# Two output products as pairs of 64-row matmuls in a hybrid decoder step

## The chip, the cores and the metric

The kernel runs on one core of a Trainium2 chip. The time is that of one execution on the device, in microseconds (us). Times of engines, waits and transfers come from one profiled execution. The engines are PE (matrix products; its weight loads are listed as PEld), DVE and ACT (element-wise work, both can read the accumulator memory PSUM), POOL (element-wise work in SBUF) and SP (which issues most DMAs).

## The reference

One inference step of a two-layer decoder trunk in float32, for one prompt of 512 tokens and for 8 sample sequences of 8 tokens each; the model width is 1024. Cut to what matters:

```python
# layer 0
xr, yg = split(h @ rnn_w_in, 2)
xr = causal_dwconv(xr)                                  # width 4
o = rg_lru(xr)                                          # gates, then a recurrence over the tokens
x = x + g1 * ((o * gelu(yg)) @ rnn_w_out)               # output product of the recurrent block
x = x + g2 * swiglu(modulate(rms_norm(x)))
kv = modulate(rms_norm(x)) @ w_kv                       # shared keys and values
# layer 1
q = rope(modulate(rms_norm(x)) @ attn_w_q)
x = x + g1 * (sliding_sink_attention(q, k, v) @ attn_w_o)   # output product of the attention
x = x + g2 * swiglu(modulate(rms_norm(x)))
y = rms_norm(x)
```

Shift, scale and gate of each norm (`sh`, `sc`, `g`) come from a conditioning vector through a large product (`ada`). The outputs are the two `y`, and the convolution, recurrence and key/value states.

## The kernel before, in words

The residual stream is kept transposed, model columns on partitions and tokens along the free dimension: `x[h]` with 8 blocks (`KC`) of 128 model columns. The tokens are in two column halves `h` (called A and B), each of 288 columns (`HC`): 256 prompt tokens (`HP`) and 4 sample sequences of 8 tokens.

A product with float32 accuracy is made from three products in the reduced type float32r. Each operand v is split into `hi`, v rounded to float32r, and `lo`, v - hi rounded; `product` (lines 1032 to 1040) adds hi x hi, hi x lo and lo x hi for each of the 8 blocks of 128 rows: 24 matmuls of 128 rows, 128 weight columns and 288 token columns, all into one PSUM bank. Weights arrive by DMA as `raw`, and ACT and DVE split them into two `wh` buffers (`convert`, line 1006). `linear` (line 1049) makes a job of such a product and an evacuation function, for one block of 128 output columns; each job runs once per column half.

The two output products of the change are of this kind: 8 jobs with `rnn_w_out` (line 1214), whose moving operands are pairs of `sl` buffers, and 8 jobs with `attn_w_o` (line 1814), whose moving operands lie in `h`. Their evacuation is `residual` (line 1058): one DVE instruction multiplies 256 columns of the bank with the gate and adds them to `x`, a second multiplies the 32 sample columns, POOL adds those, and ACT squares the new block for the next norm. After the last block the norm of that half follows (`norm_f`, line 918), and then the SwiGLU products.

PSUM has eight banks: six for products and transposes (`NMM`, tag `mm`), two for the `ada` products and the attention outputs. `td` is a set of four scratch buffers of SBUF.

No instruction is issued when the Python code reaches it. Every call is recorded (line 489, which is why all instructions carry that line), with a cost from a table (`Engine.record`, lines 430 to 489). `Recorder.schedule` (line 227) is a planner: it plays the five engines against each other, takes for each the recorded instruction that can start first with a bonus for those early in the code, and may look ahead of the oldest one that is still open by `WIN` places. It knows banks and buffers in use, and adds 100 ns where PE goes from one matmul `mode` to another (line 339). The resulting order is written out engine by engine; on the chip each engine runs its list in order and waits for semaphores.

Matmuls of fewer than 128 rows exist already in one place that matters here: the attention scores (line 1623) take 64 rows of a head from the upper or the lower half of the partitions, two by two, in plain float32.

Of the kernel before, what the change touches and what calls it, by code (L numbers as in the profile page):

```python
# [13 lines left out]
F32R = mybir.dt.float32r  # L14
BF16 = mybir.dt.bfloat16
AF = mybir.ActivationFunctionType
ALU = mybir.AluOpType
AX = mybir.AxisListType

P = 128  # L20
D = 1024
KC = D // P
# [5 lines left out]
HC = 288  # L28
# [18 lines left out]
MK = "4 V VVG S VVG"  # L47
MQ = "4 V VVG SSSV VG"
SPW = 60
WIN = 600  # L50

RNN = "x0 x1 x2 g0 g1 x3 y0 y1 x4 g2 g3 x5 y2 x6 y3 g4 g5 x7 y4 y5 g6 g7 y7 y6"
ATT = "q0A q2A a0A q1A q0B a2A q1B q3A a0B q2B q4A a1A a1B a4A a3A q3B a2B q5A q4B a3B q6A a5A q5B q7A a6A a4B s0A q6B a5B s1A s2A s3A q7B a7A s0B fA s2B a6B a7B s1B o0A s3B o1A o2A fB"
# [8 lines left out]
SH1, SC1, G1, SH2, SC2, G2 = range(6)  # L62
KVSH, KVSC = 6, 7
L1 = 8
# [356 lines left out]
class Engine:  # L421
# [8 lines left out]
    def record(self, name, args, kw):  # L430
        eng, obj = self.eng, self.obj
        outs, ins, vals = [], [], list(args) + list(kw.values())
        isap = lambda v: hasattr(v, "ap") and hasattr(v, "tensor")
        first = kw["out"] if "out" in kw else args[0]
        outs.append(first)
        if isap(kw.get("accum_out")):
            outs.append(kw["accum_out"])
        ins = [v for v in vals if isap(v) and not any(v is o for o in outs)]
        f = max([_free(x) for x in outs + ins])
        scal = len([x for x in ins if x is not kw.get("accum_out") and _free(x) == 1 and len(x.ap) <= 2 and f > 1])  # L440
        ps_ = any(_is_psum(x) for x in ins)
        func, lat = None, 0

        reads = [x for x in (list(args) if "out" in kw else list(args[1:])) + [v for n, v in kw.items() if n not in ("out", "accum_out")] if isap(x)]
        wide = [x for x in reads if not _is_psum(x) and not str(x.space).endswith("DRAM") and (_free(x) > 1 or f == 1)]
        port = eng == "POOL" and name != "dma_start" and bool(wide) or eng == "DVE" and not ps_ and (len(wide) > 1 or name == "tensor_scalar" and f > 1)
        port = (2 if eng == "POOL" and f <= 40 else 1) if port else 0
        mode = 0
        if name == "matmul":
            if kw.get("start") is not True:  # L450
                ins.append(first)
            n = _free(first)
            dt = args[2].dtype
            cost = max(n + 32, 264) / 2.4 if dt == F32R else max(214.0 if first.ap[0][1] > 32 else 134.0, n * 4 / 2.4)
            if dt == F32 and 64 in (first.ap[0][1], args[1].ap[0][1]) and n >= P:

                mode = 1 if args[1].ap[0][1] == 64 else 2
                cost = n * 2 / 2.4 + 20
            if first.ap[0][1] == 32 and args[1].ap[0][1] == P and n >= P:
                cost = n / 2.4 + 6  # L460
                mode = 3
        elif name == "transpose":
            cost = 107.0
        elif name == "dma_start":
            src = args[1]
            n = max(_free(first) * first.ap[0][1], _free(src) * src.ap[0][1])
            cost, lat = (460.0 if eng == "SP" else 1020.0), n * 4 / 335.0 + 5
        elif eng == "ACT":
            cost = (52 if ps_ else 94) + 0.8333 * f + (0, 90, 187)[min(scal, 2)] + (96 if isap(kw.get("accum_out")) else 0)
            func = str(args[2]).split(".")[-1] if name == "activation" else "Copy"  # L470
        elif eng == "DVE":
            if name == "reciprocal":
                cost = 62 + 6.28 * f
            elif name == "memset":
                cost = 20 + 0.5 * f
            elif name == "tensor_tensor_scan":
                cost = 70 + 2.1 * f
            else:
                cost = 67 + 1.0417 * f + (61 if scal and name == "scalar_tensor_tensor" else 0)
        else:  # L480
            if name == "tensor_tensor":
                cost = 150 + (165 if ALU.pow in vals else 2.4) * f
            elif name == "memset":
                cost = 35 + 0.83 * f
            elif name == "tensor_scalar":
                cost = 260 + 3.33 * f if scal else 95 + 1.05 * f
            else:
                cost = 120 + 3.3 * min(f, 32) + max(f - 32, 0) * 1.1
        self.rec.add(eng, lambda: getattr(obj, name)(*map(real, args), **{k: real(v) for k, v in kw.items()}), cost, outs, ins, func, lat, port, mode)  # L489
# [26 lines left out]
def trunk_kernel(ctx, tc, a):  # L516
    nc = tc.nc
    rec = Recorder(a["shadow"])
    V, S, G, T, Q = (Engine(rec, n, o) for n, o in (("DVE", nc.vector), ("ACT", nc.scalar), ("POOL", nc.gpsimd), ("PE", nc.tensor), ("SP", nc.sync)))
# [10 lines left out]
    def ps(pool=pmm, tag="mm"):  # L530
        cnt[0] += 1
        return rec.tile(pool, tag, NMM if tag == "mm" else (8 - NMM), RMM if tag == "mm" else 1, [P, 512], F32, f"{tag}{cnt[0]}")
# [12 lines left out]
    td = Slots(rec, cp, "td", SLOT, NTD)  # L545
# [28 lines left out]
    @contextmanager  # L574
    def early(n):

        rec.bias -= n
        yield
        rec.bias += n
# [338 lines left out]
    def norm_f(gsc, gsh):  # L918

        def f(h):  # L920
            with early(EN):
                stats(h)
                H[h] = hkind[h](F32R)
                V2[h] = [sl() for _ in range(KC)]
                v = h4r(h)
                s, u = ta(), tb()
                xs, us = [y.f[:, 0 : 32 * KC].rearrange("p (c n) -> p c n", c=KC) for y in (s, u)]
                x4, u4 = [y.rearrange("p c (b t) -> p c b t", b=4) for y in (xs, us)]
                sam = [mods[:, g, :, 1 + 4 * h : 5 + 4 * h].unsqueeze(3).to_broadcast([P, KC, 4, NT]) for g in (gsc, gsh)]
                V.tensor_tensor(xs, x[h][:, :, HP:HC], rstd[h][:, HP:HC].unsqueeze(1).to_broadcast([P, KC, 32]), ALU.mult)  # L930
                V.tensor_tensor(u4, x4, sam[0], ALU.mult)
                V.tensor_tensor(u4, u4, sam[1], ALU.add)
                s.done()
                for c in range(KC):
                    S.copy(V2[h][c].f[:, HP:HC], us[:, c, :])
                u.done()
                for c in range(KC):
                    t = ta()
                    n, y = t.f[:, 0:HP], V2[h][c].f
                    V.tensor_tensor(n, x[h][:, c, 0:HP], rstd[h][:, 0:HP], ALU.mult)  # L940
                    S.activation(y[:, 0:HP], n, AF.Identity, bias=mp(gsh, c), scale=mp(gsc, c))
                    t.done()
                    split(v[:, c, 0, :], v[:, c, 1, :], y[:, 0:HC])
        return f
# [87 lines left out]
    def product(o, u, ops, first=True, last=True):  # L1032
        n = u.kc
        hi, lo = u.hi.r, u.lo.r
        for k in range(n):
# [3 lines left out]
            T.matmul(o, hi[:, ks], xl, start=False, stop=False)  # L1039
            T.matmul(o, lo[:, ks], xh, start=False, stop=(last and k == n - 1))  # L1040

    class Job:
        def __init__(self, cost, run, need=(), drops=(), after=None):
            self.cost, self.run, self.need, self.drops, self.after = cost, run, need, drops, after
# [2 lines left out]
    jobs, stages = [], []  # L1047

    def linear(u, ops, evac, after=None):
        def run(h):  # L1050
            o = ps()
            product(o[:, 0:HC], u, ops(h))
            with early(ER):
                evac(h, o)
        jobs.append(Job(0.369 * u.kc, run, (u,), (u,), after))


    def residual(h, o, c, g, last):
        xp, xs = x[h][:, c, 0:HP], v48(x[h][:, c, HP:HC])
        V.scalar_tensor_tensor(xp, o[:, 0:HP], mp(g, c), xp, ALU.mult, ALU.add)  # L1060
        t = ta()
        V.tensor_tensor(v48(t.f[:, 0:32]), v48(o[:, HP:HC]), msam(g, c, h), ALU.mult)
        (V if g == L1 + G2 and c == KC - 1 else G).tensor_tensor(xs, xs, v48(t.f[:, 0:32]), ALU.add)
        t.done()
        if last and (g != L1 + G2 or c < KC - 1):
            square(h, c)
# [125 lines left out]
    for i, w in enumerate(seq_):  # L1192
        c = int(w[1:])
# [18 lines left out]
    norm_f0 = norm_f(SC2, SH2)  # L1212

    for m in range(KC):
        linear(
            unit_cols(a["rnn_w_out"][0], m * P),
            lambda h: [(s0.r[:, 0:HC], s1.r[:, 0:HC]) for s0, s1 in RN[h]],
            lambda h, o, m=m: residual(h, o, m, G1, True),
            rnn_done if m == KC - 1 else None,
        )  # L1220

# [248 lines left out]
    jobs = []  # L1470
# [99 lines left out]
    kvjobs, jobs = jobs, []  # L1570
# [14 lines left out]
    for c in range(KC):  # L1585
# [5 lines left out]
        u = Unit(KC, srcs)  # L1591
# [210 lines left out]
    jobs = []  # L1802
    stages.append([(j, h) for h in range(2) for j in kvjobs])
    wo = a["attn_w_o"][0]
    for m in range(KC):
        srcs = []
        for gp in range(2):
            for j in range(2):
                r0 = (8 * gp + 4 * j) * 64
                srcs.append((slice(64 * j, 64 * j + 64), slice(4 * gp, 4 * gp + 4), ALL,  # L1810
                             wo[r0 : r0 + 256, m * P : (m + 1) * P].rearrange("(l d) n -> d l n", d=64)))
        u = Unit(KC, srcs)
        units.append(u)
        linear(u, hops, lambda h, o, m=m: residual(h, o, m, L1 + G1, True), norm_f(L1 + SC2, L1 + SH2) if m == KC - 1 else None)


    each = []
# [242 lines left out]
```

## Time and profile before

| | |
|---|---|
| two timed runs | 1261.37 and 1262.76 us, median 1262.07 us |
| span of the profiled execution | 1261.1 us |
| recurrent output product, first to last matmul on PE | about 161 to 236 us |
| attention output product, first to last matmul on PE | about 788 to 858 us |
| mean TensorE clock granted | 0.998 |
| HBM | 160.85 MB read, 131 GB/s over the span with writes |

The profiled execution is given by its span, from the first to the last instruction; the timed runs are measured from outside and lie within 2 us of it. In the rows of the profile an instruction is named by what it writes and reads, buffer numbers left out, then by its rows x columns of the array (128\*128, or 64\*128 for half the rows) and by its operand's shape; float32r operands of PE are listed as f32. After the count of a group come busy time, mean duration and the idle time of the engine in front of it. In a timeline row the first number is the start of a run of like instructions, the second the time until the last of them ends.

### The profile page before, as it was taken

The numbers are of one execution on the slowest core, as the hardware profiler recorded it, in microseconds if no ns is written. First come the engines' busy times: TensorE is split into PE (matmuls) and PEld (weight loads), VectorE is DVE, ScalarE is ACT, GpSimd is POOL, SyncE is SP. The second block draws the span as 40 slices with busy tenths as digits, with TensorE's granted clock in tenths as the row PEclk, the third lists the DMA queues.
The fourth block names the chain that finished last, engine by engine and source line by source line (L and its number), as shares of the span: only waits on it lengthen the run. The fifth ranks groups of instructions, "written<-read, shape, count | busy, mean of one in ns | idle before, by whom it ended". The sixth has DMA issues, their size and how long they took to land.

```text
span 1261.1 us, 25732 instructions
## 1 busy us (share of the span) xinstructions
PE 1246.3 (99%) x9704; PEld 1182.5 (94%) x9704; DVE 883.6 (70%) x2157; ACT 650.3 (52%) x1464; POOL 494.2 (39%) x709
## 2 busy tenths in 40 slices
PE   9999999999999999999999999999999999999997
PEld 8889899899998998999999987999999999999997
DVE  6887985875574675467569878558757758756856
ACT  4797873752352354145358678538425425524522
POOL 3475751131551552345135436110435346435511
PEclk9999999999999999999999999999999999999999
DMA  9956555516646556445424321322333323323222
GB/s 306 306 188 204 171 181 151 162 50 212 195 139 180 180 161 194 158 147 146 126 68 86 72 60 57 95 84 96 87 97 86 101 85 97 97 77 100 81 88 76
DMA packets 223982, 165.42 MB, mean 131 GB/s; under 512 B 23757, under 2 KB 209065, under 8 KB 223826
## 3 DMA queue, kind: packets, MB, share of 16 engines
q1 hardware_dynamic: 223410, 163.45, 43.5%
q8 instruction: 76, 1.25, 0.4%
q14 instruction: 48, 0.39, 0.1%
q0 software_dynamic: 448, 0.32, 0.1%
HBM read 160.85 MB, written 4.87 MB: 131 GB/s over the span
## 4 chain that ended last, share of the span: by engine, by line
PE 88%; ACT 5%; DVE 3%; DMA 2%; POOL 1%; issue 1%; SPq 0%; ACTq 0%; DVEq 0%
PE mm L489 84%; PE ada L489 4%; DMA wh<-in_ada_w_dram 1%; ACT h L489 1%; ACT ta L489 1%; ACT tb L489 1%; DVE sl L489 1%; ACT sl L489 1%; DVE ta L489 1%; DMA raw<-in_rnn_w_in_dram 1%; DVE wh L489 1%; ACT wh L489 1%; SPq L489 0%; ACT td L489 0%; ACT L489 0%
## 5 line engine op out<-in xcount | busy, mean ns | idle before, releaser
L489 PE MATMUL mm<-h,wh 128*128 128x288 f32 x4128 | 591.4, 297 | 1.8 <-ACT wh L489 0.7
L489 PEld LDWEIGHTS mm<-h,wh 128*128 128x128 f32 x4128 | 559.3, 188 | 16.8 <-issue 6.0
L489 PE MATMUL mm<-sl,wh 128*128 128x288 f32 x3218 | 463.1, 296 | 0.3 <-ACT sl L489 0.3
L489 PEld LDWEIGHTS mm<-sl,wh 128*128 128x128 f32 x3218 | 437.3, 188 | 10.0 <-issue 5.9
L489 ACT CAST wh<-raw 128x512 fp32r<-128x512 f32 (+3 forms) x388 | 267.8, 711 | 304.6 <-PE mm L489 212.1
L489 DVE TENSOR_TENSOR wh<-raw,wh 128x512 fp32r<-128x512 f32 (+3 forms) x388 | 340.5, 900 | 63.9 <-ACT wh L489 59.6
L489 POOL TENSOR_TENSOR raw<-raw 128x512 f32<-128x512 f32 x76 | 109.4, 1439 | 178.0 <-DVE wh L489 147.2
L489 POOL TENSOR_TENSOR x<-x,ta 128x32 f32<-128x32 f32 x152 | 56.6, 372 | 298.8 <-DVE ta L489 297.0
L489 DVE SCALAR_TENSOR_TENSOR x<-mm,mods,x 128x256 f32<-128x256 f32 x160 | 77.2, 483 | 132.4 <-PE mm L489 131.2
L489 POOL TENSOR_TENSOR raw<-raw,raw 128x512 f32<-128x512 f32 x76 | 112.5, 1480 | 3.5
L489 PE MATMUL mm<-tb,wh 128*128 128x288 f32 (+1 forms) x488 | 88.2, 296 | 0.7 <-DVE td L489 0.6
L489 POOL TENSOR_TENSOR td<-td,td 128x288 f32<-128x288 f32 x38 | 31.9, 841 | 114.4 <-ACT td L489 114.4
L489 PEld LDWEIGHTS mm<-tb,wh 128*128 128x128 f32 x488 | 72.6, 188 | 1.3 <-DVE td L489 0.9
L489 ACT ACTIVATE ta<-x 128x288 f32<-128x288 f32 x56 | 24.6, 444 | 68.1 <-POOL x L489 63.0
L489 PE MATMUL mm<-ta,wh 128*128 128x288 f32 (+1 forms) x254 | 55.7, 297 | 0.0
L489 DVE TENSOR_TENSOR td<-mm,td 128x288 f32<-128x288 f32 x76 | 33.6, 454 | 28.6 <-PE mm L489 28.5
L489 PE MATMUL ada<-reg,cz 128*32 128x512 f32 (+1 forms) x448 | 48.3, 552 | 0.0
L489 DVE TENSOR_TENSOR sl<-td,sl 128x288 fp32r<-128x288 f32 x50 | 38.8, 777 | 8.6 <-ACT sl L489 8.2
L489 PEld LDWEIGHTS mm<-ta,wh 128*128 128x128 f32 x254 | 41.5, 188 | 1.7 <-ACT ta L489 1.7
L489 ACT COPY td<-mm 128x256 f32<-128x256 f32 (+1 forms) x102 | 33.5, 357 | 13.9 <-PE mm L489 13.9
L489 ACT CAST sl<-ta 128x288 fp32r<-128x288 f32 x54 | 23.4, 433 | 31.8 <-DVE ta L489 29.4
L489 ACT ACTIVATE ta<-ta,stat 128x256 f32<-128x256 f32 (+2 forms) x72 | 32.5, 474 | 9.6 <-DVE stat L489 9.3
(207 smaller groups left out, 1272.2 us busy)
## 6 DMA issues: line engine op xcount, KB each, us to landing
raw<-in_ffn_w_in_dram SPq DMA_DIRECT2D x88, 512.0 KB
reg<-in_ada_w_dram SPq DMA_DIRECT2D x80, 512.0 KB
raw<-in_ffn_w_out_dram SPq DMA_DIRECT2D x32, 384.0 KB
raw<-in_ffn_w_out_dram SPq DMA_DIRECT2D x32, 320.0 KB
raw<-in_rnn_w_in_dram SPq DMA_DIRECT2D x16, 512.0 KB
reg<-in_kv_ada_w_dram SPq DMA_DIRECT2D x16, 512.0 KB
wh<-in_ada_w_dram SPq DMA_DIRECT2D x24, 256.0 KB
raw<-in_rnn_w_out_dram SPq DMA_DIRECT2D x8, 512.0 KB
```

Of the source, the lines that this page charges most:

```text
L489: self.rec.add(eng, lambda: getattr(obj, name)(*map(real, args), **{k: real(v) for k, v in kw.items()}), cost, outs, ins, func, lat, port, ...
```

## The change

Each of the 24 matmuls of the two output products becomes two matmuls of 64 rows: rows 0 to 63 go into a bank `o`, rows 64 to 127 into a second bank `p`, in turn. ACT then copies `p` to an SBUF buffer, DVE adds `o` and the copy into another, and the residual reads that one in place of the bank. The planner prices a 64-row float32r matmul at (n + 6) / 4.8 ns and gives it mode 1, that of the 64-row float32 ones. `WIN` goes from 600 to 500. The other products are as before.

```diff
-WIN = 600
+WIN = 500
...
+            if dt == F32R and args[1].ap[0][1] == 64:
+                cost, mode = (n + 6) / 4.8, 1
...
+    def product_rows(os_, u, ops):
+        n = u.kc
+        hi, lo = u.hi.r, u.lo.r
+        for k in range(n):
+            xh, xl = ops[k]
+            ks = slice(k * P, (k + 1) * P)
+            for i, (w, v) in enumerate(((hi, xh), (hi, xl), (lo, xh))):
+                for o, r in zip(os_, (slice(0, 64), slice(64, P))):
+                    T.matmul(o, w[r, ks], v[r], start=k + i == 0, stop=k == n - 1 and i == 2)
...
+    def linear_rows(u, ops, c, g, after=None):
+        def run(h):
+            o, p = ps(), ps()
+            product_rows((o[:, 0:HC], p[:, 0:HC]), u, ops(h))
+            with early(ER):
+                y, s = td(), td()
+                S.copy(s.f[:, 0:HC], p[:, 0:HC])
+                V.tensor_tensor(y.f[:, 0:HC], o[:, 0:HC], s.f[:, 0:HC], ALU.add)
+                s.done()
+                residual(h, y.f, c, g, True)
+                y.done()
+        jobs.append(Job(0.369 * u.kc, run, (u,), (u,), after))
...
-        linear(
+        linear_rows(
             unit_cols(a["rnn_w_out"][0], m * P),
             lambda h: [(s0.r[:, 0:HC], s1.r[:, 0:HC]) for s0, s1 in RN[h]],
-            lambda h, o, m=m: residual(h, o, m, G1, True),
+            m,
+            G1,
             rnn_done if m == KC - 1 else None,
         )
...
-        linear(u, hops, lambda h, o, m=m: residual(h, o, m, L1 + G1, True), norm_f(L1 + SC2, L1 + SH2) if m == KC - 1 else None)
+        linear_rows(u, hops, m, L1 + G1, norm_f(L1 + SC2, L1 + SH2) if m == KC - 1 else None)
```

## The prediction

> **What bounds the kernel now.** I read the page first: shares of each engine, clock, the chain that ended last and the costliest groups.
>
> ```profile
> span 1261.1 us, 25732 instructions
> PE 1246.3 (99%) x9704; PEld 1182.5 (94%) x9704; DVE 883.6 (70%) x2157; ACT 650.3 (52%) x1464; POOL 494.2 (39%) x709
> ...
> PEclk9999999999999999999999999999999999999999
> ...
> PE 88%; ACT 5%; DVE 3%; DMA 2%; POOL 1%; issue 1%; SPq 0%; ACTq 0%; DVEq 0%
> ...
> L489 PE MATMUL mm<-h,wh 128*128 128x288 f32 x4128 | 591.4, 297 | 1.8 <-ACT wh L489 0.7
> ...
> L489 PE MATMUL mm<-sl,wh 128*128 128x288 f32 x3218 | 463.1, 296 | 0.3 <-ACT sl L489 0.3
> ```
>
> PE is busy for 99% of the span at the full clock, it is 88% of the chain, and its two large groups waited 2.1 us in all. PE's own issue rate is the bound; DVE, ACT and DMA matter only where they make PE wait. So an edit to PE's stream counts one for one, and work added on ACT and DVE costs nothing until PE waits for it. A busy PE is not yet PE at its peak, so next I looked at how far apart its matmuls start. The 297 ns of a record overlap the next ones; the step is read from the timeline.
>
> ```profile
> 200.22 11.85 PE L489 MATMUL mm<-sl,wh 128*128 128x288 f32 x88
> ...
> 85.50 0.44 PE L489 MATMUL mm<-ta,wh 128*128 128x300 f32 x2
> ...
> 87.14 0.42 PE L489 MATMUL mm<-h,wh 128*128 128x288 f32 x2
> ...
> 118.91 0.44 PE L489 MATMUL mm<-ta,wh 128*128 128x300 f32 x2
> ...
> 120.57 0.29 PE L489 MATMUL mm<-h,wh 128*128 128x288 f32 x1
> ```
>
> The first row lies inside the recurrent output product: 88 matmuls, 87 steps and one last duration, (11.85 - 0.297)/87 = 0.1328 us a step. The gate matmuls have 300 columns; between the quoted rows lie twelve each time: 1.64/12 = 0.137 and 1.66/12 = 0.138, mean 0.1375. Twelve more columns cost 0.0047 us, 0.39 ns a column. At that rate 288 columns stream in about 0.113 us, and some 0.02 us of each step is not streaming. That is what halves could recover. With rounding of 0.01 us at each start the rate has an error near 0.08 ns, so 0.46 ns (all streaming, nothing to recover) isn't excluded.
>
> **The pairs.** The change takes out 768 matmuls (two products, 8 column blocks, 2 column halves, 24 each) and adds 1,536 of 64 rows, in pairs with different row halves. The kernel already has such pairs, in float32: the attention scores, where every matmul of the code is two records.
>
> ```profile
> 714.12 0.60 PE L489 MATMUL mm<-wh,sl 64*128 64x256 f32 x4
> 714.34 1.25 PE L489 MATMUL mm<-wh,sl 64*128 64x256 f32 x12
> 714.55 0.60 PE L489 MATMUL mm<-wh,sl 64*128 64x256 f32 x6
> 714.77 0.60 PE L489 MATMUL mm<-wh,sl 64*128 64x128 f32 x6
> 714.99 0.60 PE L489 MATMUL mm<-wh,sl 64*128 64x256 f32 x4
> 714.55 0.63 PEld L489 LDWEIGHTS mm<-wh,sl 64*128 64x128 f32 x8
> ```
>
> These are the timeline's answers for narrow stretches, each starting at another pair; the third column is the count. Pairs of 256 columns start at 714.12, 714.34 and 714.55, so a pair takes 0.215 us; 714.77 to 714.99 holds two pairs of 128, 0.11 us each. The 128 further columns cost 0.105 us, 0.82 ns a column, about twice the 0.39 ns above: float32 streams at half the rate of the float32r products, and both halves of a pair stream together. What a pair takes beyond its streaming is 0.11 - 0.105 = 0.005 us, between 0 and 0.006 with rounding. The eight weight loads, four pairs, end within 0.63 us, so loads of the two halves overlap too.
>
> For a float32r pair: 288 columns at half of 0.82 to 0.84 ns are 0.118 to 0.121, plus the handover: 0.122 to 0.126, and I take 0.124. Per matmul replaced 0.1328 - 0.124 = 0.0088, times 768: **-6.8 us** (-8.3 to -5.2).
>
> The row speaks against a rule of the Trainium skill, "TensorE: Matmul & The Clock Gate", section on LDWEIGHTS: a load's time goes by its columns and not its rows, P / 1.2 ns, so half the rows cost as much as all; two loads of 128 columns in turn would need some 213 ns a pair, an estimate from that page, and make this change lose some 60 us. The page "TensorEngine Tiling (Array Packing)", section Key Properties, lets different tiles load and compute in parallel, and the 0.11 us pair with two loads of 128 columns agrees with that one.
>
> **Changes of shape.** PE pays whenever it goes between the whole array and halves. A visit in the trace:
>
> ```profile
> 702.01 0.83 PE L489 MATMUL mm<-h,wh 128*128 128x288 f32 x5
> 702.76 1.58 PE L489 MATMUL mm<-wh,sl 64*128 64x128 f32 x16
> 704.27 0.53 PE L489 MATMUL mm<-h,wh 128*128 128x288 f32 x2
> ```
>
> Five whole ones ought to take 0.664, and the halves start after 0.75: +0.09. The halves are four pairs of 128 and four of 256, 4 x 0.11 + 4 x 0.215 = 1.30, and whole ones start after 1.51: +0.21. The first whole step is 0.53 - 0.297 = 0.233 instead of 0.133: +0.10. In and out cost 0.40 us, 0.20 a change. (The same Key Properties say that a change of tiling mode drains the engine; these rows put 0.20 us on it.) In the changed program's instruction order I count 250 changes of shape on PE, against 229: the halves stand in 18 stretches, from 1 to 478 long, and strictly alternate but for a handful. 21 x 0.20 = **+4.2 us** (0.17 to 0.22 each: 3.6 to 4.6).
>
> **Evacuation.** Each of the 32 products now needs a copy of one bank on ACT and an add on DVE ahead of the residual.
>
> ```profile
> L489 ACT COPY td<-mm 128x288 f32<-128x288 f32 x38 | 15.1, 398 | 9.1 <-PE mm L489 9.1
> L489 DVE TENSOR_TENSOR td<-mm,td 128x288 f32<-128x288 f32 x76 | 33.6, 454 | 28.6 <-PE mm L489 28.5
> L489 ACT ACT_TABLE_LOAD x19 | 24.4, 1283 | 7.3 <-DVE stat L489 3.9 <-DMA raw<-in_c_sample_dram 3.2
> core 0: us, PE busy (x) PEld busy (x) DVE busy (x) ACT busy (x) POOL busy (x), PEclk, DMA share, GB/s
> 162.00:180.00 18.00, 17.96 (x135) 16.08 (x135) 14.63 (x31) 16.15 (x27) 7.96 (x17) 1.00 0.48 146
> 200.00:227.00 27.00, 27.00 (x206) 25.00 (x205) 15.24 (x37) 10.71 (x27) 3.55 (x8) 1.00 0.39 117
> 800.00:830.00 30.00, 29.94 (x241) 28.53 (x238) 15.61 (x44) 11.18 (x27) 2.65 (x9) 1.00 0.33 95
> PE mm L489 <- ACT sl L489: 0.3, 1, 0.3
> ```
>
> That is 32 x 0.398 = 12.7 us of ACT and 32 x 0.454 = 14.5 us of DVE. In the body of the two stages (200 to 227, 800 to 830) both engines are idle for two fifths or more, and one product in 3 us brings them 0.4 and 0.45: hidden. The residual then reads SBUF instead of PSUM, same size: nothing. At the end of a column half the chain to its norm grows by 0.85 us and two handovers; PE's cover is the other half's products or the first FFN matmuls of the half that is ahead, several us in the new order. I take 0, at worst some 1 us at each of the two stage ends. ACT also loads three more tables (22 for 19, from the order), 3.8 us on an engine at half load.
>
> The window of the planner (WIN, 500 for 600) reorders everything slightly. With PE's waits this small there is little to win: -1.5 to +2 with the stage ends, value 0.
>
> **Sum.** -6.8 + 4.2 = -2.6. The page's span is 1261.1, and the two timed runs' median of 1262.07 lies 0.97 above; I leave that as it is: 1262.07 - 2.6 = 1259.5 us. With its bounds this case goes from -8.3 + 3.6 - 1.5 = -6.2 to -5.2 + 4.6 + 2 = +1.4: 1256 to 1263.5.
>
> **Rivals.** (1) *No handover to recover.* If the 0.02 us belong to float32r rather than to the whole-array shape, or are streaming at 0.46 ns a column, a pair takes the 0.1328 of a whole matmul and, from the 0.005 above, some 0.002 for starting its second half: 0.135. For: the 300-column rows exclude this only weakly, and no float32r pair is in the trace. Against: float32 pairs lose at most 0.006. Price 768 x 0.0022 + 4.2 = +5.9, 1268. The change breaks even at a pair of 0.1273 us.
>
> (2) *Halves load or run in turn.* One mechanism, in each of the 768 pairs: the second half waits for the first, as by the weight-load rule above. If float32r halves don't overlap, a pair is at least the two loads in turn, 2 x 0.11 = 0.22: 768 x 0.087 + 4.2 = +71, 1333 us. It decides for slower by 2% (25 us) from a pair of 0.160 on. Against: the float32 pairs. For: float32r delivers results twice as fast per half, and both halves write PSUM at once.
>
> (3) *Too few banks.* There are six banks for products. Before, PE bridged the wait for the last recurrent operands (162 to 182 us, ACT 16.15 of 18 us busy) by opening six products of one bank and finishing them later, and waited only 0.3 us. With two banks a product it can open three, so up to two products' worth of work, 2 x 24 x 0.133 = 6.4 us, is missing as cover: 1259.5 + 6.4 = 1266. Against: the new order moves products of the input stage in between, as if to cover it.
>
> (4) *The change doesn't do what it says* would be pairs that the planner pulls apart; the order shows they stay together, so no chance is set aside.
>
> **The numbers.** Forecast 0.58, (1) 0.18, (3) 0.14, (2) 0.10. The range takes in the forecast's own 1256 to 1263.5 and reaches into (1) and (3): 1255 to 1269; left out are (2) and the far tails of the others. A measurement of this kernel tells some 2% (25 us) from no change: slower by that only in (2) and a little of combined mishaps, 0.10; faster would need pairs below 0.10 us, 0.01; within 2%: 0.89.
>
> **What will show it.** In the profile after: pairs in the product stages stepping by 0.122 to 0.126 us (a stretch of 2n halves lasting n times that); 0.2 us lost at each change to and from halves; weight loads of a pair starting together; PE waits on ACT or DVE between 160 and 240 and at 780 to 870 still below 2 us. I am wrong if pairs step by 0.133 or more, if PE waits for a bank or for the recurrent operands for several us, or if other stages move by more than 2 us through the new order.

## The result and the profile after

The changed kernel takes 1276.26 us (median of 1276.22 to 1276.31) against 1262.07 us: 1.0115 times the time before, interval 1.0086 to 1.0144. That is 14.2 us slower; the forecast was 2.6 us faster, with a range that ended at 1269. The interval lies clear of 1, so the kernel is slower, by less than the 2% that the prediction takes as its limit. The span of its profiled execution is 1274.5 us, 13.4 us longer. Its page, the lines that answer to those shown of before:

```profile
span 1274.5 us, 27323 instructions
PE 1256.2 (99%) x10472; PEld 1188.7 (93%) x10472; DVE 897.9 (70%) x2189; ACT 663.9 (52%) x1499; POOL 496.2 (39%) x709
...
PEclk9999999999999999999999999899999999999999
...
PE 87%; DVE 5%; ACT 3%; DMA 2%; issue 1%; POOL 1%; SPq 0%; ACTq 0%; DVEq 0%; POOLq 0%
...
L491 PE MATMUL mm<-h,wh 128*128 128x288 f32 (+1 forms) x4512 | 596.5, 299 | 6.3 <-ACT wh L491 2.7
...
L491 PE MATMUL mm<-sl,wh 128*128 128x288 f32 (+1 forms) x3602 | 461.4, 295 | 0.0
```

PE still is the bound at 99%. DVE works 14.3 us more (883.6 to 897.9; 14.5 were worked out) and ACT 13.6 (650.3 to 663.9; 12.7 for the copies and 3.8 for three table loads). New are an 8 in the clock row and 6.3 us of idle time in front of the `h,wh` group, which had 1.8. A slice of that row is 32 us wide, so I asked for PE's waits and then for the windows in which the clock was lowered. First the waits (engine and what it waited for; us in all, times, longest):

```profile
PE mm L491 <- ACT wh L491: 2.7, 2, 1.9
PE mm L491 <- ACT h L491: 1.7, 1, 1.7
PE mm L491 <- DVE td L491: 1.7, 3, 0.7
PE mm L491 <- POOL tst L574: 1.4, 1, 1.4
PE mm L491 <- DVE wh L491: 1.4, 1, 1.4
```

All rows of that view add up to 10.8 us, those of before to 7.5. The waits of 1.9 (ACT `wh`, from 820.4 us on), 1.7 (ACT `h`, from 254.0) and 1.4 us (DVE `wh`, from 160.6) weren't in the kernel before. Now the windows of the kernel after; the columns are the stretch, its length, busy time and count of PE, PEld, DVE, ACT and POOL, the granted clock, the DMA share and GB/s:

```profile
158.94:162.35 3.41, 1.99 (x15) 0.98 (x8) 3.41 (x7) 1.73 (x5) 3.27 (x8) 1.00 0.00 0
162.35:165.77 3.42, 3.42 (x17) 3.42 (x16) 3.42 (x8) 0.43 (x1) 3.42 (x8) 0.50 0.51 153
667.53:670.94 3.41, 2.67 (x21) 2.43 (x21) 3.41 (x9) 2.79 (x5) 2.98 (x3) 1.00 0.44 100
670.94:674.35 3.41, 3.41 (x16) 3.41 (x16) 1.72 (x4) 1.82 (x4) 1.80 (x1) 0.50 1.23 212
817.70:821.10 3.40, 2.68 (x16) 1.66 (x14) 1.75 (x6) 1.22 (x5) 0.00 (x0) 1.00 0.02 5
821.13:827.95 6.82, 5.63 (x44) 5.42 (x46) 2.24 (x5) 1.78 (x4) 0.25 (x1) 0.50 0.56 161
```

Three times PE runs at half its clock, 3.41 + 3.41 + 6.82 = 13.65 us, each time behind a window in which it stood still for a while; PE still counts as busy for 1.99 to 2.68 us of these windows. Before had no such stretch between its first matmuls and its last few microseconds. The pairs themselves, in the timeline of the kernel after (start, duration, count of halves):

```profile
199.83 21.36 PE L491 MATMUL mm<-sl,wh 64*128 64x288 f32 x320
...
822.32 34.78 PE L491 MATMUL mm<-h,wh 64*128 64x288 f32 x478 [1.93 <-ACT wh L491]
```

The first row is 160 pairs at full clock: (21.36 - 0.293)/159 = 0.1325 us a pair, against 0.1328 for a whole matmul. The second holds a part of the half-clock stretch at 821.

### The profile page after: what moved, and what is told of

Its sections match the earlier page's. It is cut to its first block, busy times and chain, and to the rows that moved or that the text cites. A ratio compares the mean times of both kernels' runs of the same rounds, so it can differ in the third digit from the quotient of the medians.

```text
span 1274.5 us, 27323 instructions
## 1 busy us (share of the span) xinstructions
PE 1256.2 (99%) x10472; PEld 1188.7 (93%) x10472; DVE 897.9 (70%) x2189; ACT 663.9 (52%) x1499; POOL 496.2 (39%) x709
## 4 chain that ended last, share of the span: by engine, by line
PE 87%; DVE 5%; ACT 3%; DMA 2%; issue 1%; POOL 1%; SPq 0%; ACTq 0%; DVEq 0%; POOLq 0%
PE mm L491 83%; PE ada L491 4%; DVE sl L491 2%; DVE ta L491 1%; DVE wh L491 1%; DMA wh<-in_ada_w_dram 1%; ACT tb L491 1%; ACT sl L491 1%; DMA raw<-in_rnn_w_in_dram 1%; ACT wh L491 1%; ACT h L491 1%; DVE h L491 0%; ACT ta L491 0%; SPq L491 0%; DVE tb L491 0%
## 5 line engine op out<-in xcount | busy, mean ns | idle before, releaser
L491 PE MATMUL mm<-h,wh 128*128 128x288 f32 (+1 forms) x4512 | 596.5, 299 | 6.3 <-ACT wh L491 2.7
L491 PEld LDWEIGHTS mm<-h,wh 128*128 128x128 f32 (+1 forms) x4512 | 564.8, 190 | 22.1 <-issue 8.2
L491 PE MATMUL mm<-sl,wh 128*128 128x288 f32 (+1 forms) x3602 | 461.4, 295 | 0.0
L491 PEld LDWEIGHTS mm<-sl,wh 128*128 128x128 f32 (+1 forms) x3602 | 436.9, 187 | 9.8 <-issue 6.5
L491 DVE TENSOR_TENSOR wh<-raw,wh 128x512 fp32r<-128x512 f32 (+3 forms) x388 | 344.1, 909 | 51.7 <-ACT wh L491 46.5
L491 POOL TENSOR_TENSOR x<-x,ta 128x32 f32<-128x32 f32 x152 | 64.0, 421 | 296.8 <-DVE ta L491 296.6
L491 DVE SCALAR_TENSOR_TENSOR x<-mm,mods,x 128x256 f32<-128x256 f32 x128 | 61.8, 483 | 105.6 <-PE mm L491 104.7
L491 DVE TENSOR_TENSOR td<-mm,td 128x288 f32<-128x288 f32 x108 | 48.0, 453 | 45.0 <-PE mm L491 27.8
L491 ACT COPY td<-mm 128x288 f32<-128x288 f32 (+2 forms) x134 | 46.6, 366 | 37.3 <-PE mm L491 34.6
L491 DVE TENSOR_TENSOR sl<-td,sl 128x288 fp32r<-128x288 f32 x50 | 38.0, 760 | 10.6 <-ACT sl L491 10.1
L491 ACT COPY ta<-mm 128x288 f32<-128x288 f32 (+1 forms) x50 | 18.8, 377 | 34.7 <-PE mm L491 34.5
```

## The experiments

Times and ratios are against runs of the kernel before on the same chip.

**e1, e2, e3: window and banks apart from halves.** e1 is the kernel before with the planner's window alone changed, e2 the changed kernel with the window put back; e3 has the changed kernel's two banks, copy and add, but whole matmuls: the first four row blocks go into `o`, the other four into `p`.

```diff
 # e1, on the kernel before
-WIN = 600
+WIN = 500
 # e2, on the changed kernel
-WIN = 500
+WIN = 600
 # e3, on the changed kernel
-                for o, r in zip(os_, (slice(0, 64), slice(64, P))):
-                    T.matmul(o, w[r, ks], v[r], start=k + i == 0, stop=k == n - 1 and i == 2)
+                b = o if k < n // 2 else p
+                T.matmul(b, w[:, ks], v, start=k % (n // 2) + i == 0, stop=k % (n // 2) == n // 2 - 1 and i == 2)
```

> The kernel before with only the planner's window at 500 instead of 600. Theory A (the loss comes from the halves: no time won per pair, about 4 us of shape changes, the rest PE waits and the half-clock stretches that follow them, all made by the new products): 1260 to 1264 us, no stretch of half clock that the kernel before doesn't have. Rival B (the smaller window makes the new waits): 1267 us or more, with PE waits above 3 us in all around 160 and 820 us.

> The changed kernel with the window back at 600. Theory A: still slower than before by 6 us or more (4 us of shape changes, and waits somewhere): 1268 to 1280 us. Rival B: the waits go with the window, 1264 to 1267 us (only the shape changes are left).

> The changed kernel, but with whole 128-row matmuls: blocks 0 to 3 of a product into the first bank, 4 to 7 into the second, then the same copy and add; window 500. No halves and none of their shape changes, the same two banks and the same evacuation. If the halves themselves cost nothing but their shape changes and the planner's price for them, and banks and evacuation are hidden: 1260 to 1265 us. If two banks a product and the longer evacuation make PE wait: 1268 us or more, with a wait of over 1 us near 160 or 820 us.

e1: 1263.98 us, 1.0008 [0.9998, 1.0018]: the window alone is not told from nothing. e2: 1284.63 us, 1.0174 [1.0159, 1.0189]: with the old window the halves are worse still, above the 1268 to 1280 that I expected. e3: 1265.12 us, 1.0018 [1.0009, 1.0028], at the upper edge of the 1260 to 1265 for hidden banks and evacuation, with one half-clock stretch of 3.41 us: window, banks, copy and add together cost some 2.5 us, and the other 11 or 12 come with the halves.

**e4: steps by themselves.** A bench that leaves out the reference's computation: series of 48 matmuls or pairs without waits. Its core:

```python
def whole(n, w, v, count, cols=P):
    for i in range(count):
        k = (i % 8) * P
        mm(bank[0][0:cols, 0:n], w[:, k : k + cols], v[:, 0:n], start=i == 0, stop=i == count - 1)
def halves(n, w, v, count):
    for i in range(count):
        k = (i % 8) * P
        for o, r in zip(bank[1:3], HALF):
            mm(o[:, 0:n], w[r, k : k + P], v[r, 0:n], start=i == 0, stop=i == count - 1)
```

> Not the reference's computation: only series of 48 matmuls after one another on PE, whole (128 rows) and in pairs of halves, float32r, of 128 to 512 columns, then bfloat16 and float32; all outputs but a corner are zeros. Theory T1 (a float32r matmul pays a fixed 0.012 to 0.013 us beside its streaming of 0.417 ns a column, and a pair of halves pays it too): whole and pairs step alike, 0.133 at 288, 0.173 at 384, 0.226 at 512. T2 (float32r streams at 0.461 ns a column, nothing fixed): 0.118 at 256, 0.177 at 384, 0.236 at 512, in pairs too. T3 (the 0.1326 of a pair is the two weight loads of the halves in turn, alike by chance): pairs stay at 0.13 from 128 to 288 columns, and are faster than whole ones at 384 and 512. In all three a float32 pair steps by half of what two whole ones take.

The groups of the bench, shapes kept apart (count, busy us, mean ns of one; `aank` takes whole matmuls, `bank` one half of each pair, `dank` halves of one kind in succession; `xr` is float32r, `xb` bf16, `xf` float32):

```profile
L44 PE MATMUL aank<-xf,wf 128*128 128x288 f32 x48 | 11.9, 408 | 0.0
L50 PE MATMUL bank<-xf,wf 64*128 64x288 f32 x48 | 11.9, 405 | 0.0
...
L44 PE MATMUL aank<-xr,wr 128*128 128x384 f32 x48 | 8.5, 334 | 0.0
...
L44 PE MATMUL aank<-xr,wr 128*96 128x288 f32 x48 | 6.6, 297 | 0.0
L44 PE MATMUL aank<-xr,wr 128*128 128x288 f32 x48 | 6.5, 294 | 0.0
L50 PE MATMUL bank<-xr,wr 64*128 64x288 f32 x48 | 6.5, 291 | 0.0
...
L44 PE MATMUL aank<-xb,wb 128*128 128x288 bf16 x48 | 6.1, 286 | 0.0
L50 PE MATMUL bank<-xb,wb 64*128 64x288 bf16 x48 | 6.1, 283 | 0.0
...
L44 PE MATMUL aank<-xr,wr 128*128 128x256 f32 x48 | 5.9, 283 | 0.0
...
L44 PE MATMUL aank<-xr,wr 128*128 128x128 f32 x48 | 5.5, 274 | 0.0
...
L56 PE MATMUL dank<-xr,wr 64*128 64x288 f32 x24 | 3.3, 291 | 0.0
```

A step is busy time less one duration, over one less than the count. A whole float32r step of 288 columns is (6.5 - 0.294)/47 = 0.132 us, and a pair (6.5 - 0.291)/47 = 0.132 as well; the rounding of the busy time leaves 0.001 open. From 256 to 384 columns the step grows from 0.1195 to 0.1737, 0.42 ns a column. At that rate 288 columns stream in 0.121 us: the streaming that I forecast is right, and about 0.011 us is left over. The pair pays that left-over like the whole matmul. It isn't the length of the weight load: 96 weight columns in place of 128 make the step no shorter, (6.6 - 0.297)/47 = 0.134. It goes with the type: the bf16 step of the same size is 0.124 and has only 0.003 left over, and there too the pair, 0.124, saves nothing. Float32 as well has no gain to show, 0.2445 a record both ways. Halves of one kind in succession take 0.131 each (3.3 less 0.291 over 23): these do run one after the other, and the pairs do not.

Here the Trainium skill has the smaller figure: "TensorE: Matmul & The Clock Gate", the section "Wait — 56ns, not 53.3ns?", puts a fixed 2.5 ns on each matmul beside its columns. The bf16 step agrees with it; for float32r the bench shows four times as much.

**e5, e6: one product alone.** Halves in the recurrent product only (e5: the attention product calls `linear` as before), or in the attention product only (e6: the recurrent one does).

```diff
 # e5
-        linear_rows(u, hops, m, L1 + G1, norm_f(L1 + SC2, L1 + SH2) if m == KC - 1 else None)
+        linear(u, hops, lambda h, o, m=m: residual(h, o, m, L1 + G1, True), norm_f(L1 + SC2, L1 + SH2) if m == KC - 1 else None)
 # e6
-        linear_rows(
+        linear(
             unit_cols(a["rnn_w_out"][0], m * P),
             lambda h: [(s0.r[:, 0:HC], s1.r[:, 0:HC]) for s0, s1 in RN[h]],
-            m,
-            G1,
+            lambda h, o, m=m: residual(h, o, m, G1, True),
```

> Halves in the recurrent output product alone (384 pairs), the attention output product as before; the planner's window 500; 240 shape changes on PE against 229 before and 250 in the changed kernel. Theory 1 (a float32r pair costs what a whole step costs; the loss is 0.2 us for each shape change, about 1.3 us for the window, and longer PE waits that drop the clock): pairs still at 0.132 to 0.133 us, 11 x 0.2 = 2.2 us of shape changes, 1264 without a half-clock stretch and 1266 to 1270 if the wait near 160 us and its half-clock stretch are there. Theory 2 (pairs save 0.0088 us each as I forecast, and something else, such as the two stages disturbing each other, costs the time): 384 x 0.0088 = 3.4 us less, 1261 or 1262. With the run of the attention product alone: if the two excesses add up to about 13 to 15 us, the loss lies in each stage by itself.

> Halves in the attention output product alone (384 pairs), the recurrent output product as before; the planner's window 500; 239 shape changes. Theory 1 (pairs gain nothing; shape changes, window, PE waits with half-clock stretches): 10 x 0.2 = 2.0 us of shape changes, 1264 without a half-clock stretch, 1267 to 1271 if the wait of about 2 us between 800 and 830 us is there again with its 6.8 us at half clock; no half-clock stretch near 160 us. Theory 2 (pairs save 0.0088 us each): 1261 or 1262, the stretch of halves below 0.126 us a pair.

e5: 1271.40 us, 1.0067 [1.0052, 1.0082], 1.4 us above the top of theory 1's range, with the wait of 1.7 us for ACT `h` (at 255 us) and half-clock stretches of 3.41 us near 164 and 672. e6: 1270.11 us, 1.0058 [1.0043, 1.0073], with the wait of 2.0 us for ACT `wh` and stretches of 3.41 and 6.83 us near 665 and 815. The two excesses, 8.5 and 7.3 us, add up to 15.8, a little above the 14.2, and each alone has the window's share in it. So each product loses by itself, and neither gains anything; the stretches near 672 and 665 us lie outside both stages.

**e7: the planner's price put right.** The measured pair in its cost model:

```diff
-                cost, mode = (n + 6) / 4.8, 1
+                cost, mode = (n + 28) / 4.8, 1
```

> The changed kernel, with one number in the planner's cost model altered: a half of n columns priced at (n + 28) / 4.8 ns, 0.132 us a pair, in place of (n + 6) / 4.8, 0.1225; the order of the work follows from it, and PE has 252 shape changes. Theory A (the planner took pairs for cheaper than they are, so PE runs late by its plan and the waits and half-clock stretches come from that): the waits of 1.5 to 2 us are gone, granted clock back to 0.998, 1264 to 1268. Theory B (the waits come from two banks a product and the added copy and add, or from the tightness of the stage ends, whatever the price): waits and half-clock stretches stay, 1273 to 1280. By either, no less than 1262 + 23 x 0.2 = 1266.7 less the 1 us or so by which orders differ.

1281.05 us, 1.0143 [1.0126, 1.0160], 1 us above even theory B's range. Theory A falls: PE's waits grew to 14.2 us in all; the largest two rows, where the first was 1.7 us in the changed kernel:

```profile
PE mm L491 <- ACT h L491: 4.4, 2, 2.7
PE mm L491 <- ACT wh L491: 2.7, 2, 1.9
```

A wrong price of the pair is not by itself what makes PE wait.

**e8: a change of shape, and a standstill, by themselves.** A second bench, which also leaves out the reference's computation. Its core:

```python
for size, groups in ((48, 2), (24, 4), (8, 12), (4, 24)):
    for g in range(groups):
        whole(288, wr, xr, size)
        halves(288, wr, xr, size)
...
for copies in (1, 2, 3, 4, 5, 6):
    for rep in range(3):
        # 150 whole matmuls, `copies` ScalarE copies in a chain, one matmul that reads the last copy
```

> A bench by itself: it leaves out the whole of the reference's computation and runs float32r matmuls of 288 columns. First 96 whole ones, then 96 pairs of halves, then both in turn in groups of 48, 24, 8 and 4 (96 whole ones and 96 pairs each time, with 4, 8, 24 and 48 changes of shape). Then stretches of 150 whole matmuls (20 us), each followed by a wait for 1 to 6 ScalarE copies in a chain, three times for each number, so that PE stands still for some 0.7 to 3 us. Theory 1: each change of shape costs 0.2 us over 0.132 us a step, whatever the length of the group: the four mixed blocks take 0.8, 1.6, 4.8 and 9.6 us more than the same work unmixed. Rival: a change costs nothing between float32r shapes, and the 0.2 us is of the float32 scores alone: the four blocks take the same time within 0.3 us. On the clock: if PE standing still for 1 to 2 us is enough for a half-clock stretch of 3.4 or 6.8 us, the granted clock shows 0.5 after waits of that length and not after the shortest; if the dips of the changed kernel have another cause, the clock stays at 1.0 after all waits below 3 us.

The timeline, in the part with groups of four (`aank` whole, `bank` the first half of each pair):

```profile
130.11 0.79 PE L45 MATMUL aank<-xr,wr 128*128 128x288 f32 x4
130.83 0.40 PE L51 MATMUL bank<-xr,wr 64*128 64x288 f32 x1
...
131.55 0.40 PE L45 MATMUL aank<-xr,wr 128*128 128x288 f32 x1
```

Four whole matmuls and four pairs take 131.55 - 130.11 = 1.44 us. Eight steps of 0.132 are 1.056, so the two changes cost 0.384, 0.19 each. Groups of eight start at 102.53 and 105.04: 2.51 - 16 x 0.132 = 0.40, 0.20 each. With the step read from the starts in the trace to one more place, 0.1317 us, a change costs 0.20 us in groups of 4, 8, 24 and 48 alike: the length of the group does not matter. Then the standstills, in the timeline and in windows before and behind them:

```profile
334.09 19.91 PE L78 MATMUL fank<-xr,wr 128*128 128x288 f32 x150
355.46 0.40 PE L83 MATMUL hank<-gap,wr 128*128 128x288 f32 x1 [1.47 <-ACT gap L81]
...
377.55 0.40 PE L83 MATMUL hank<-gap,wr 128*128 128x288 f32 x1 [1.93 <-ACT gap L81]
377.79 21.46 PE L78 MATMUL gank<-xr,wr 128*128 128x288 f32 x150
...
424.81 0.40 PE L83 MATMUL hank<-gap,wr 128*128 128x288 f32 x1 [1.93 <-ACT gap L81]
425.04 19.91 PE L78 MATMUL fank<-xr,wr 128*128 128x288 f32 x150
```

```profile
330.80:334.21 3.41, 1.94 (x15) 1.71 (x14) 0.00 (x0) 1.26 (x3) 0.00 (x0) 1.00 0.00 0
375.20:378.61 3.41, 1.48 (x12) 1.25 (x11) 0.00 (x0) 1.69 (x4) 0.00 (x0) 1.00 0.00 0
378.61:382.03 3.42, 3.42 (x16) 3.42 (x16) 0.00 (x0) 0.00 (x0) 0.00 (x0) 0.50 0.02 5
423.00:426.41 3.41, 1.60 (x12) 1.61 (x13) 0.00 (x0) 1.66 (x4) 0.00 (x0) 1.00 0.00 0
443.47:446.88 3.41, 1.48 (x12) 1.25 (x10) 0.00 (x0) 1.71 (x5) 0.00 (x0) 1.00 0.00 0
446.88:450.29 3.41, 2.94 (x12) 2.94 (x13) 0.00 (x0) 0.42 (x1) 0.00 (x0) 0.50 0.00 0
```

No wait up to 1.47 us lowered the clock (nine waits). Of three waits of 1.93 us two did and one did not; all six waits of 2.4 and 2.9 us did. The windows say why waits of one length differ: the half-clock stretches start a whole number of times 3.413 us apart (378.61 to 446.88 is 20 times), so they lie on a fixed grid, and in this bench a stretch follows a grid window in which PE was busy for 1.48 us, not one with 1.60 or more. A wait that a border of the grid cuts in two can pass. The stretches of the changed kernel lie on such a grid too: from 162.35 to 670.94 us are 149 steps, from there to 821.13 another 44. A border falls at 162.35 + 27 x 3.413 = 254.5, inside the wait of 1.7 us from 254.0 on, and no stretch follows that one. The price is in the rows of 150 matmuls: 21.46 - 19.91 = 1.55 us for each 3.41 us at half clock.

The border of 1.48 to 1.60 us doesn't carry over to the kernels, whose windows also hold matmuls of other sizes. e1 has the wait for DVE `wh` too, 1.38 us from 161.6 on, so that wait comes with the planner's window of 500 and not with the halves (e2, halves with the window of 600, doesn't have it). It lies whole in one grid window, 321 steps ahead of e1's last half-clock stretch at 1256.71:

```profile
161.03:164.44 3.41, 2.03 (x15) 1.79 (x14) 3.41 (x5) 0.64 (x2) 3.35 (x7) 1.00 0.03 8
```

The clock stays up behind these 2.03 us, and in the changed kernel it falls behind 1.99 us at 158.94, with the same wait. What the chip counts in a window is not shown by these runs; the busy time of PE alone is not it.

The page "TensorE: Matmul & The Clock Gate" of the Trainium skill, section "Part 1: The HAM clock gate (the "warmup" mystery)", has that grid: a free-running window of 3413 ns. It lets the clock fall after an idle window, and the section "HAM oscillation — how this bites in real kernels" warns of idle gaps above some 3.4 us; in this bench 1.93 us was enough, and the measurement decides.

**e9, e10: fill the waits.** 33 matmuls whose results are overwritten, ahead of two of those that PE waits at; beside it the changed kernel again.

```diff
+        if n == 5173:                       # the wait near 667 us
+            for _ in range(5):
+                mm(o, *self.last[-1], start=True, stop=True)
...
+        if n == 6299:                       # the wait near 820 us; 6298 is held back until here
+            for _ in range(14):
+                for b, wv in zip((p, o), self.last[-2:]):
+                    mm(b, *wv, start=True, stop=True)
```

> The changed kernel with 33 more matmuls on PE, put ahead of two of the matmuls that PE waits at, in place of standing still: 5 whole ones at the wait of 0.74 us near 667 us, 14 pairs of halves at the wait of 1.9 us near 820 us. They repeat earlier operands into banks that the following product starts anew, so nothing that is computed changes, and the waits themselves end no sooner. Theory A (standing still is what makes the clock fall for the next 3.4 or 6.8 us): the half-clock stretches at 671 and 821 are gone, the one at 162 stays, 10.24 us less at half clock, about 5 us less in time: 1270 to 1272. Theory B (the clock falls for another reason, such as the change of shape or the stage, or PE working harder): the stretches stay, and the time is 1276 to 1278.

> The changed kernel unaltered, on the same chip as the run with the added matmuls, for a comparison side by side: 1275 to 1277, half-clock stretches near 162, 671 and 821 us, 13.65 us together.

e9: 1275.06 us (1271.34 to 1275.73), 1.0095 [1.0079, 1.0112], between the two theories' ranges. e10: 1276.12 us, 1.0112 [1.0095, 1.0129], with three stretches of 3.41 us, 10.24 us in all and not the 13.65 that I expected: the one near 820 us is half as long as in the first profile of the same kernel. In e9 the stretches at both filled places are gone, as theory A says. But another came, in windows of e9:

```profile
788.21:791.62 3.41, 3.08 (x21) 2.10 (x20) 3.20 (x10) 2.93 (x15) 2.08 (x6) 1.00 0.27 72
791.62:795.04 3.42, 3.42 (x16) 2.17 (x17) 1.90 (x12) 1.63 (x7) 1.20 (x5) 0.50 0.68 201
```

PE counts as busy for 3.08 us ahead of it, with matmuls of 64 to 256 columns from the attention. So it isn't standing still alone. e10's grid window from 786.38 us on, in the same part of the kernel, has 3.02 us of PE busy and the clock stays up behind it; that where the grid lies decides is likely, but not shown. My 5 us were too much; the difference of the two medians is 1.1 us, within the spread of e9's runs. Even one kernel varies in this: e9's fastest execution, 1271.34 us, had a mean granted clock of 0.998, its other three 0.996.

**e11, e12: plan pairs as one instruction.** e11 gives the planner each pair as one instruction with a whole matmul's price and shape; e12 does the same, but with the shape of halves, so that a change costs 0.1 us in the plan.

```diff
 # e11; e12 has mode 1
-                cost, mode = (n + 6) / 4.8, 1
+                cost, mode = max(n + 32, 264) / 4.8, 0
...
-                for o, r in zip(os_, (slice(0, 64), slice(64, P))):
-                    T.matmul(o, w[r, ks], v[r], start=k + i == 0, stop=k == n - 1 and i == 2)
+                with rec.together():
+                    for o, r in zip(os_, (slice(0, 64), slice(64, P))):
+                        T.matmul(o, w[r, ks], v[r], start=k + i == 0, stop=k == n - 1 and i == 2)
```

> The changed kernel, but the planner takes each pair of halves as one instruction with the price of a whole matmul (0.133 us) and without a price for the change of shape, so that it plans as it does for whole matmuls in two banks; the halves then cause 273 changes of shape on PE (225 with whole matmuls in two banks, 250 in the changed kernel). Theory 1 (halves cost their changes of shape, 0.2 us each, and the long waits come from the planner's view of halves): 48 x 0.2 = 9.6 us over the 1265 of whole matmuls in two banks, 1273 to 1276, with PE waits near 8.5 us in all as there. Rival (the long waits and the half-clock stretches come with the halves whatever the plan): 1278 or more, PE waits above 11 us, stretches near 821 us. Forecast's theory (a pair saves 0.0088 us): 1268 to 1270.

> As the run before it, but a pair, still one instruction of 0.133 us for the planner, is given the shape of halves, so that the planner pays 0.1 us for each change of shape and makes fewer: 244 on PE, 15 more than before. Theory 1 (pairs gain nothing, 15 x 0.2 = 3.0 us of shape changes; two banks with copy, add and window some 2.5 us; the long waits come from planning the halves one by one): 1266 to 1269, PE waits below 9 us, at most one half-clock stretch. Rival (the waits come from the price of a shape change or from halves as such): 1272 or more, with waits near 2 us at 250 or 820 us and two or more half-clock stretches.

e11: 1274.35 us, 1.0097 [1.0080, 1.0114], inside theory 1's 1273 to 1276, with 9.0 us of waits (e3: 8.5) and one stretch near 246 (e3: 243). Beside e3 it is the cleanest comparison of the study, whole matmuls against pairs in nearly one plan. Two stretches of 119 steps each, pairs in the timeline of e11 and whole matmuls in that of e3:

```profile
180.80 16.00 PE L491 MATMUL mm<-sl,wh 64*128 64x288 f32 x238
```

```profile
178.90 16.15 PE L491 MATMUL mm<-sl,wh 128*128 128x288 f32 x119
```

The median of the steps inside these rows is 0.132 us in both, so nothing is lost or won in the pairs. The kernels differ by 1274.35 - 1265.12 = 9.2 us; less the 0.5 us of longer waits that is 8.7 us for 48 more changes of shape, 0.18 each. e12: 1269.30 us, 1.0059 [1.0044, 1.0074], 7 us faster than the changed kernel and still slower than before. It is just past the top of theory 1's range, with 10.6 us of waits where I had allowed 9. That is hardly less than the changed kernel's 10.8: the 7 us are three half-clock stretches (3 x 1.55) and six changes of shape (1.2) less. Against e7, which has nearly the same price but plans the halves one by one, the waits fall from 14.2 to 10.6 us; one of 1.7 us near 815 stays, with the only half-clock stretch behind it.

## Why the prediction was wrong

Two terms of the sum failed. With the pairs at what they measured and all else as forecast, the sum would have been 1262.07 - 0.2 + 4.2 = 1266.1 us, inside the range; the other 10 us up to 1276.26 are waits and half clock, which the sum put at 0.

**What bounds the kernel**: right. PE stayed at 99%, and DVE's and ACT's additions of 14 us each lie beside it.

**The pairs**: the first step that failed. "What a pair takes beyond its streaming is 0.11 - 0.105 = 0.005 us" was measured on float32 pairs and carried to float32r, and the 0.02 us that float32r steps take beyond streaming were put down to the whole-array shape. e4 splits them: streaming is 0.121 us (forecast 0.118 to 0.121), the rest some 0.011, and it goes with float32r, in halves as in whole matmuls. I had no whole float32 step to set beside it; e4 has one, and there too the pair saves nothing, so the small handover of the float32 pairs was no sign of what pairing does. The term of -6.8 us measured 768 x (0.1325 - 0.1328) = -0.2. That is rival (1), whose condition ("if the 0.02 us belong to float32r") holds; its pair of 0.135 was 0.0025 too dear, because the second half costs nothing extra. Its 1268 us lacks the waits and the clock as the forecast does. The break-even of 0.1273 us was the right test, and 0.1325 is on the losing side.

**Changes of shape**: right, +4.2 us. The 0.20 us read from one visit in the scores came out at 0.20 in e8 for float32r and at 0.18 between e3 and e11.

**Evacuation** and the window: hidden for the most part, but not 0. Together with the second bank they are the 2.5 us of e3, somewhat above the top of "-1.5 to +2 with the stage ends"; e3's one half-clock stretch is some 1.6 us of it. The three more table loads don't show on PE.

**Waits and clock**: the second step that failed, and the larger. PE's waits grew by 3.3 us, above my bound of 2; and I priced a wait at its own length, while a wait of 0.7 to 2 us can also take 1.55 us or twice that from the matmuls behind it. With four times 3.41 us at half clock that is 6.2 us, at most: PE was busy for only 5.63 of the 6.82 us at 821. Put together for each kernel: changes of shape over the 229 of before at 0.2, stretches of 3.41 us at 1.55, the waits of the view over 7.5, against the span over 1261.1.

| kernel | changes | stretches | waits | sum, us | measured, us |
|---|---|---|---|---|---|
| after | 21: 4.2 | 4: 6.2 | 3.3 | 13.7 | 13.4 |
| e1 window alone | 0 | 0 | -0.1 | -0.1 | 1.0 |
| e2 old window | 21: 4.2 | 5: 7.8 | 5.8 | 17.8 | 22.2 |
| e3 whole, two banks | -4: -0.8 | 1: 1.6 | 1.0 | 1.8 | 3.1 |
| e5 recurrent alone | 11: 2.2 | 2: 3.1 | 2.3 | 7.6 | 8.5 |
| e6 attention alone | 10: 2.0 | 3: 4.7 | 1.1 | 7.8 | 7.4 |
| e7 pair repriced | 23: 4.6 | 4: 6.2 | 6.7 | 17.5 | 18.4 |
| e9 filled | 21: 4.2 | 2: 3.1 | 1.2, and 2.5 of added matmuls | 11.0 | 12.8 |
| e10 after again | 21: 4.2 | 3: 4.7 | 3.7 | 12.6 | 13.0 |
| e11 planned as whole | 44: 8.8 | 1: 1.6 | 1.5 | 11.9 | 11.9 |
| e12 planned as a pair | 15: 3.0 | 1: 1.6 | 3.1 | 7.7 | 7.3 |

The sum has no term for the pairs and comes within 1.3 us of all but e9, where 1.8 us stay open, and e2, where it is 4 us.

**The other rivals**: (2) halves in turn is out; a pair takes 0.132 us and two halves of one kind 2 x 0.131. (3) too few banks is out as the main cause: e3 has the same two banks a product, and its waits are 1.0 us longer than before, not 6.4. Its place was wrong too; the long waits near 160, 254 and 820 us are for operands from ACT and DVE.

What stays open: why the plan with halves makes PE wait longer for ACT than the plan with whole matmuls. The pair's price alone is excluded (e7); planning halves one by one looks like a part of it (e12 against e7). The planner also takes 0.1 us for a change that costs 0.2; that price wasn't tried alone. No kernel of the study beats the one before, and with pairs that gain nothing, none with halves has a reason to.

## What to carry to other kernels

Split a step into streaming and the rest, and before counting on the rest, measure it for the same type and the same shapes: a small cost in one type says nothing of another. Count changes of array shape as a cost of their own, 0.2 us here, since a halving that gains nothing per pair still pays them. Where PE is the bound, price a wait of some 1.4 us or more, or a shorter one beside small matmuls, at up to its length plus 1.55 us for each half-clock stretch of 3.41 us, of which one or two followed here. Expect that to move with every reordering, since it hangs on where the work falls on the grid.

## What was not expected of the hardware

A float32r matmul costs about 0.011 us beside its columns where a bf16 one of the same size costs 0.003, and below 256 columns its step hardly shrinks: 0.111 us at 128 columns, 0.1195 at 256. The wait of 0.74 us near 667 us was in the kernel before as well, at 661, without a half-clock stretch; after, a grid window held all of it together with twelve matmuls of one column, and one followed.
